# A conditional expert block placed one expert group earlier, in other scratch, and four fewer constant products

## The chip, the cores and the metric

The kernel runs on one core of a Trainium2 chip. The metric is the device time of one execution in microseconds (us). The engines of a core are named as in the profile: PE is the matrix engine (PEld its weight loads), DVE the vector engine, ACT the scalar engine, POOL the general engine and SP the engine that issues nearly all transfers (DMAs). A "q" behind a name is that engine's instruction sequencer.

## The reference, cut to what matters

One decoder layer: a layer norm, a mixer (two branches, gated and summed), a second norm, and a mixture of experts over 256 tokens. The experts stand in 4 groups of 8, and each token goes to two of them. The end of the layer is what this case is about:

```python
for gi in range(N_GROUPS):
    hid = (jax.nn.silu(jnp.einsum("td,edf->tef", t, expert_w_gate[gi]))
           * jnp.einsum("td,edf->tef", t, expert_w_up[gi]))
    hid = hid * combine[:, gi, :, None].astype(hid.dtype)
    y = y + jnp.einsum("tef,efd->td", hid, expert_w_down[gi])
...
h = layer_norm(DEEPNORM_ALPHA * h + ffn, ln2_g[i], ln2_b[i])
```

D_MODEL is 1024 and the inner width of an expert 256, in float32. So each of the 32 experts has 3 MB of weights: gate and up (1 MB each) and down (1 MB).

## The kernel before, in words

The first part of the program (to about 330 us) is the mixer and the router. The second part handles the experts. Each expert gets a row of slots for the tokens that were sent to it, and the experts are worked on four at a time: `units` has eight groups of four, and `four(u)` is called for u = 0 to 7 (the sixth group is u = 5, the seventh u = 6, the last u = 7).

In `four(u)`, `gate_up` (L1273) multiplies the first 32 slots of four experts at once by their gate and up weights (tile `gu`). The four experts alternate matrix by matrix, so the fourth matmul already needs the last of the four experts. `activate` (L1304, L1305), `turn` (L1312, L1313) and `down` (L1322, tile `dn`) follow, and `scatter` (L1334) adds the result to the four output tiles `y`.

Three kinds of work are conditional. If an expert of a group has more than 32 tokens, a second pass is made over its slots 33 to 64 (`tc.If(most > QC)`, L1394 and L1440). If any expert has more than 64 tokens (`CAP`), `overflow_all()` computes the rest in a loop over all experts, with weights loaded once more into a tile `ow` and normed tokens in a tile `hT` (L1450). A branch is decided at run time by each engine for itself. The program has a path for each outcome: where a block is skipped, the engine runs a short path that adds to the semaphores what the block would have added.

Weights come in on one queue, issued by SP in the order in which the program's builder placed them; PE, ACT, DVE and POOL have their order written by hand. Every transfer counts on one of eight semaphores in turn (DMAHW0 to DMAHW7). `load_gu` and `load_dn` take their buffers in rotation through `unit`: seven buffers for `gu`, seven for tag `rd`, which is shared by the `dn` tiles, by `ow`, by `gb` (the broadcast rows of the last norm) and by the result `o`. A tile that is taken earlier moves every later tile to the next buffer. `lt` holds three scratch buffers `wr0` to `wr2`; the gathered slots `xs` of even groups lie in `wr0`, those of odd groups in `wr1`.

Behind u = 6 follow `second_rows()` (four products of L783 and four copies of L1465, which spread the norm's gain and offset over the partitions) and `warm_up(ident, NW3, "pwm3")` (L1082): NW3 products of the identity with itself, whose result nobody reads. Each is two matmuls in the trace.

Of the kernel before, what the change touches and what calls it, by code (L numbers as in the profile page):

```python
# [8 lines left out]
F32R = mybir.dt.float32r  # L9
# [8 lines left out]
P = 128  # L18
D = 1024
KT = 8  # L20
# [21 lines left out]
RT_AT = 2  # L42
XR_AT = (0, 6)
NW2 = 13
NW3 = 18
LN_EPS = 1e-5
RMS_EPS = 1e-6
ALPHA = 2.0 ** 0.25
# [3 lines left out]
def f32(ap):  # L52
    return ap.bitcast(F32)
# [24 lines left out]
def block_kernel(ctx: ExitStack, tc: tile.TileContext, io, out, dbg=None):  # L78
# [17 lines left out]
    lt = ctx.enter_context(late_cm)  # L96
# [713 lines left out]
    def unit(tag, name):  # L810
        order = gu_order if tag == "gu" else dn_order
        k = order[taken[tag] % len(order)]
        taken[tag] += 1
        return pools[k].tile([P, 4096 if tag == "gu" else 2048], F32, name=name, tag=tag, bufs=order.count(k))

    def load_gu(*es):

        for e in es:
            if e < NE:
                raw[e] = [unit("gu", f"gu{e}").rearrange("p (a k f) -> p a k f", a=2, k=KT), None]  # L820
                for a_, nm in enumerate(("expert_w_gate", "expert_w_up")):
                    S.dma_start(raw[e][0][:, a_], io[nm][e].rearrange("(p k) f -> p k f", k=KT))

    def load_dn(*es):

        for e in es:
            if e < NE:
                raw[e][1] = unit("rd", f"dn{e}").rearrange("p (r d) -> p r d", r=2)
                S.dma_start(raw[e][1], io["expert_w_down"][e].rearrange("(p r) d -> p r d", r=2))
# [301 lines left out]
    def gather(c, k, tag):  # L1131

        pt = pm(tag, f"px{c}{k}").rearrange("p (k s) -> p k s", k=2)
        for i in range(2):
            px[c, k + i] = pt[:, i, :]
            for n in "hl":
                for t in range(2):
                    one_part(c, k + i, n, t)
# [7 lines left out]
    def gathered(c, k, eng):  # L1146
        affine(XS[:, k, c * NT:(c + 1) * NT], px[c, k], k, eng)
# [3 lines left out]
    NQ = len(units)  # L1151
# [10 lines left out]
    def slots(u, i, eng, part=0):  # L1162

        e, w = units[u][i], QC
        if i == 0:
            xsd[u, part] = f32(lt.tile([P, 1024], F32R, name=f"xs{u}{part}", tag=f"wr{(u + part) % 2 if u + part else 2}").rearrange("p (k s) -> p k s", k=KT))
        off_ = slot_at(e, eng) if e else 0
        win = XS[:, :, bass.ds(off_ + part * w, w)] if e else XS[:, :, part * w:part * w + w]
        (A.copy if eng is A else V.tensor_copy)(xsd[u, part][:, :, w * i:w * i + w], win)
# [37 lines left out]
    def rest():  # L1207

        for i in range(2):
            pt = pm("ty"[i], f"pg1s{i}")  # L1210
            row(pt, 0, i, True, True)
            for t in range(2):
                x_ = h1[t][:, i * 512:(i + 1) * 512]
                V.tensor_tensor(x_, x_, pt, op=ALU.mult)
        gap(1)

        t0 = rt("mrk0", 2, NE, at=at_pos)
        V.scalar_tensor_tensor(t0, rk, 1.0, asb, op0=ALU.add, op1=ALU.mult)
        V.tensor_scalar_add(mrk, t0, -1.0)


        ge, gp = r2("ge", NG), r2("gp")
        V.tensor_sub(ge, gl, bc(gm, [P, 2, NG]))
        A.activation(ge, ge, AF.Sigmoid, scale=-1.0)
        ws_ = []
        for i in range(2):
            w_ = r2(f"w{i}")
            A.activation(w_, dm, AF.Sigmoid, scale=(1.0, -1.0)[i])
            ws_.append(w_)
        A.activation(r2("warmed"), dm, AF.Silu)  # L1230

        for i in range(2):
            q, a = rt(f"qr{i}", 2, NE, at=at_q2 + 2 * NE * i), r2(f"rs{i}")
            V.scalar_tensor_tensor(q, rk, 1.0, AA[:, i], op0=ALU.add, op1=ALU.mult)
            V.tensor_reduce(a, q, axis=AX.X, op=ALU.add)
            for t in range(2):
                V.tensor_scalar(rhs[:, 2 * i + t, :], iot[:, :CAP], a[:, t, :], None, op0=ALU.is_equal)
        V.reciprocal(ge, ge)
        V.tensor_scalar_add(ge, ge, -1.0)
        V.tensor_reduce(gp, ge, axis=AX.X, op=ALU.add)  # L1240
        V.reciprocal(gp, gp)
        for i, w_ in enumerate(ws_):
            V.tensor_mul(w_, w_, gp)
            V.tensor_mul(CW[i], AA[:, i], bc(w_, [P, 2, NE]))

        V.tensor_add(cov, CW[0], CW[1])
        V.scalar_tensor_tensor(cov, rk, float(CAP), cov, op0=ALU.is_ge, op1=ALU.mult)
# [20 lines left out]
    def gate_up(u, part=0):  # L1268

        pgd[u, part] = pm("g", f"pg{u}{part}")  # L1270
        for k in range(KT):
            for e, c in cols_of(u):
                T.matmul(pgd[u, part][c, :], xsd[u, part][:, k, c], raw[e][0][:, :, k, :], start=k == 0, stop=k == KT - 1)  # L1273

    def weigh():

        pt = pm("y", "pcs")
        for o, c0 in ((0, 0), (NQ, QC)):
            for i in range(2):
                for t in range(2):  # L1280
                    for c in range(4):
                        T.matmul(pt[QC * c:QC * c + QC, o:o + NQ], rhs[:, 2 * i + t, c0:c0 + QC], CW[i][:, t, c::4], start=t + i == 0, stop=t + i == 2)
        V.tensor_copy(cs, pt[:, :2 * NQ])
        both = glp.tile([P, 512], F32, name="hd", tag="gl", bufs=1).rearrange("p (i r s) -> p i r s", i=2, r=2)
        hd.extend(both[:, i] for i in range(2))

    def ranks():
        prk = pm("t", "prk")
        for t in range(2):
            T.matmul(prk[:NE, t * P:(t + 1) * P], mrk[:, t, :], idb, start=True, stop=True)  # L1290
        A.copy(rkT, prk[:NE, :NT])

    def scatter_map(u, part=0):

        pt = ptd[u, part] = pm("t", f"pt{u}{part}")
        for e, c in cols_of(u):
            T.matmul(pt[c, NT:], bc(idb[:NE, e:e + 1], [NE, QC]), rkT, start=True, stop=True)  # L1297
        V.tensor_scalar(sct[(u + part) % 2], pt[:, NT:], smod[:, part:part + 1], None, op0=ALU.is_equal)  # L1298
# [37 lines left out]
    def residual_add(n, t):  # L1336

        T.matmul(y[t][n], ident, h1[t][:, n * 512:(n + 1) * 512], start=True, stop=False)
        row(y[t][n], 1, n, False, False)
# [40 lines left out]
    def next_slots(u):  # L1380
        for i in range(4):
            slots(u, i, V if i % 2 else A)

    def four(u):

        e0 = units[u][0]
        gate_up(u)
        if u == 0:
            for k, tag in ((0, "t"), (2, "y"), (4, "t"), (6, "y")):
                gather(1, k, tag)  # L1390
                for i in range(2):
                    gathered(1, k + i, A if k % 4 else V)
        most = nc.values_load(cmi[0:1, u:u + 1], engines=three, min_val=0, max_val=NT)
        with tc.If(most > QC):  # L1394
            for i in range(4):
                slots(u, i, V if i % 2 else A, 1)
            gate_up(u, 1)
        if u == 0:
            rest()
        n1 = e0 + 7  # L1400
        load_gu(*((n1, n1 + 1, n1 + 2, n1 + 3) if n1 + 4 < NE - 1 else (n1,)))
        if u == 0:
            for t in range(2):
                for n in range(2):
                    residual_add(n, t)
            load_dn(6)
            weigh()
            ranks()
        if n1 == NE - 1:
            load_dn(NE - 4, NE - 3, NE - 2)  # L1410
        scatter_map(u)
        activate(u)
        turn(u)
        if u + 1 < NQ:
            next_slots(u + 1)
            for n in range(2):
                down(u, n, "yg"[n])
            for n in range(2):
                scatter(u, n)
            second(u, most)  # L1420
        else:
            for n in range(2):
                down(u, n, "yg"[n])
            second(u, most)
            for n in range(2):
                scatter(u, n)
        if n1 + 4 < NE - 1:
            load_dn(n1, n1 + 1, n1 + 2, n1 + 3)
        else:
            load_dn(n1)  # L1430
            if n1 < NE - 1:
                load_gu(NE - 4, NE - 3, NE - 2)
        if u == NQ - 2:
            overflow_all()
            second_rows()
            warm_up(ident, NW3, "pwm3")

# [10 lines left out]
    def overflow_all():  # L1448
        most = nc.values_load(cmi[0:1, 8:9], min_val=0, max_val=NT)
        with tc.If(most > CAP):  # L1450
            ow = unit("rd", "ow")
            hT = f32(lt.tile([P, 1024], F32R, name="hT", tag="wr0").rearrange("p (k s) -> p k s", k=KT))
            for t_ in range(2):
                overflow(t_, hT, ow)

# [80 lines left out]
```

## Time and profile before

| what | us |
|---|---|
| median of 3 runs | 560.68 (558.67 to 561.95) |
| the profiled execution | 558.53 |
| its span, first to last instruction | 556.8 |
| PE busy in the span | 475.9 (85%) |
| DMA from 340 to 520 us, in windows of 10 or 20 us | 394 to 424 GB/s |

The page divides the span into 40 slices, and the views of the trace name each instruction by its line of the kernel, its engine and its tiles. All durations in the text are read from the one profiled execution.

### The profile page before, as it was taken

What the parts mean: (1) busy time and instruction counts of PE and PEld (TensorE: products, weight loads), DVE (VectorE), ACT (ScalarE), POOL (GpSimd) and SP (SyncE); (2) the same over time, 40 slices, a digit from 0 to 9 for tenths busy, and PEclk for the clock granted to TensorE, in tenths of its full rate; (3) what the DMA queues carried; (4) which work ended last, traced back from release to release, by engine and by line L of the source; (5) the groups of instructions that cost most, each with busy time, mean ns of one, the idle gap of its engine ahead of it and who ended that gap; (6) DMA issues with size and microseconds to landing.
All of it is one profiled execution on the core that took longest, in us unless ns stands there. A gap on an engine that the chain in (4) does not pass through costs nothing. (4 is left out here: it accounts for less than half of the span.)

```text
span 556.8 us, 8809 instructions
## 1 busy us (share of the span) xinstructions
PE 475.9 (85%) x3353; PEld 339.4 (61%) x3353; DVE 232.7 (42%) x516; ACT 185.0 (33%) x382; POOL 171.1 (31%) x154
## 2 busy tenths in 40 slices
PE   7898799999998998999799879886879898468681
PEld 4797788899987876789787755441222233222520
DVE  5785825663245433336995756220120101001016
ACT  2554345446545464444353412120210201101100
POOL 7492886745544355445450300000000000000002
PEclk9698999999999999999999899897999788879796
DMA  8553242233432414339879995999999999999922
GB/s 202 122 141 87 64 120 82 78 89 101 126 103 75 112 43 117 111 99 316 285 276 416 406 395 207 419 417 419 419 420 417 422 419 415 421 403 421 414 115 75
DMA packets 74582, 136.35 MB, mean 245 GB/s; under 512 B 9857, under 2 KB 59154, under 8 KB 62242
## 3 DMA queue, kind: packets, MB, share of 16 engines
q1 hardware_dynamic: 72640, 134.26, 65.5%
q10 hardware_dynamic: 1890, 1.39, 0.7%
q8 instruction: 33, 0.54, 0.4%
q14 instruction: 19, 0.16, 0.1%
HBM read 133.54 MB, written 2.10 MB: 244 GB/s over the span
## 5 line engine op out<-in xcount | busy, mean ns | idle before, releaser
L232 POOL TENSOR_TENSOR ws_in<-wr_in,ws_in 128x1024 fp32r<-128x1024 f32 x41 | 99.1, 2421 | 74.4 <-ACT ws_in L231 71.5
L236 PE MATMUL pj<-hTh,ws_in 128*128 128x256 f32 (+1 forms) x352 | 105.9, 302 | 1.7 <-ACT hTh L215 1.0
L238 PE MATMUL pj<-hTh,ws_in 128*128 128x256 f32 (+1 forms) x352 | 102.5, 292 | 0.0
L237 PE MATMUL pj<-hTl,ws_in 128*128 128x256 f32 (+1 forms) x352 | 102.2, 292 | 0.2 <-DVE hTl L216 0.2
L1273 PE MATMUL pg<-gu,xs 128*32 128x512 f32 x640 | 76.0, 604 | 11.1 <-DMA gu<-expert_w_up 7.7
L1493 POOL TENSOR_SCALAR rs<-mv 128x1 f32<-128x1 f32 x2 | 0.4, 221 | 233.4 <-DVE mv L1492 233.4
L236 PEld LDWEIGHTS pj<-hTh,ws_in 128*128 128x128 f32 x352 | 68.1, 194 | 4.0 <-issue 1.4
L237 PEld LDWEIGHTS pj<-hTl,ws_in 128*128 128x128 f32 x352 | 67.8, 193 | 1.5 <-issue 0.9
L238 PEld LDWEIGHTS pj<-hTh,ws_in 128*128 128x128 f32 x352 | 67.6, 192 | 0.8 <-issue 0.7
L1273 PEld LDWEIGHTS pg<-gu,xs 128*32 128x32 f32 x640 | 32.4, 111 | 50.3 <-issue 44.4
L1322 PE MATMUL py<-dn,hd 128*32 128x512 f32 x320 | 46.8, 717 | 12.8 <-DMA dn<-expert_w_down 7.8
L231 ACT CAST ws_in<-wr_in 128x1024 fp32r<-128x1024 f32 x44 | 45.9, 1042 | 3.1 <-DMA wr_in<-w_in 3.1
L1298 DVE TENSOR_SCALAR sc<-pt,smod 128x256 fp32r<-128x256 f32 x10 | 4.8, 484 | 99.0 <-PE pt L1297 99.0
L1326 DVE TENSOR_TENSOR yy<-py,yy 128x512 fp32r<-128x512 f32 x20 | 13.8, 692 | 63.6 <-ACT yy L1325 56.5
L1322 PEld LDWEIGHTS py<-dn,hd 128*32 128x32 f32 x320 | 10.9, 126 | 39.8 <-issue 24.2
L1334 PE MATMUL y<-yy,sc 128*128 128x512 f32 x80 | 25.8, 439 | 4.3 <-ACT yy L1325 3.0
L1304 ACT ACTIVATE gs<-pg 128x256 f32<-128x256 f32 x10 | 3.8, 384 | 76.4 <-PE pg L1273 76.4
L1334 PEld LDWEIGHTS y<-yy,sc 128*128 128x128 f32 x80 | 13.9, 194 | 21.9 <-ACT yy L1325 7.4
L1325 ACT CAST yy<-py 128x512 fp32r<-128x512 f32 x20 | 11.7, 586 | 45.5 <-PE py L1322 44.4
L729 DVE TENSOR_TENSOR_SCAN kp<-kp,one 128x144 f32<-128x144 f32 (+1 forms) x16 | 17.5, 1125 | 14.8 <-ACT kp L724 14.8
L311 DVE SCALAR_TENSOR_TENSOR qkv<-pj,cols,qkv 128x271 f32<-128x271 f32 (+2 forms) x36 | 17.8, 498 | 12.9 <-ACT qkv L309 12.3
L888 POOL TENSOR_TENSOR h<-h,gb 128x512 f32<-128x512 f32 x8 | 12.9, 1645 | 12.9 <-ACT gb L885 12.9
(539 smaller groups left out, 830.1 us busy)
## 6 DMA issues: line engine op xcount, KB each, us to landing
gu<-expert_w_gate SPq DMA_DIRECT2D x32, 1024.0 KB
gu<-expert_w_up SPq DMA_DIRECT2D x32, 1024.0 KB
dn<-expert_w_down SPq DMA_DIRECT2D x32, 1024.0 KB
wr_in<-w_in SPq DMA_DIRECT2D x44, 512.0 KB
wr_o<-w_out SPq DMA_DIRECT2D x8, 512.0 KB
wr_w_branch_dn<-w_branch_dn SPq DMA_DIRECT2D x4, 512.0 KB
wr_w_branch_sb<-w_branch_sb SPq DMA_DIRECT2D x4, 512.0 KB
h<-x SPq DMA_DIRECT2D x2, 512.0 KB
```

Of the source, the lines that this page charges most:

```text
L231: A.copy(wh, raw)
L232: (sub or V).tensor_sub(wl, raw, f32(wh))
L236: T.matmul(pt, lh, rh, start=first, stop=False)
L237: T.matmul(pt, lh, rl, start=False, stop=False)
L238: T.matmul(pt, ll, rh, start=False, stop=last)
L311: V.scalar_tensor_tensor(y[:, s:], pt[:, :L - s], ccol(3 - s, r + j), y[:, s:], op0=ALU.mult, op1=ALU.add)
L729: V.tensor_tensor_scan(k_, k_, bc(one1, [P, n]), 1.0, op0=ALU.mult, op1=ALU.mult)
L888: G.tensor_tensor(x_, x_, gb, op=op)
L1273: T.matmul(pgd[u, part][c, :], xsd[u, part][:, k, c], raw[e][0][:, :, k, :], start=k == 0, stop=k == KT - 1)
L1322: T.matmul(py[c, :], hd[(u + part) % 2][:, r, c], raw[e][1][:, r, n * 512:(n + 1) * 512], start=r == 0, stop=r == 1)
L1326: V.tensor_sub(yy[:, 1, :], py, f32(yy[:, 0, :]))
L1334: T.matmul(y[t][n], sct[(u + part) % 2][:, t * P:(t + 1) * P], yy[:, p_, :], start=False, stop=p_ == 1 and part == 0 and u == NQ - 1)
```

## The change

`overflow_all()` is called at the end of u = NQ - 3 = 5 (behind the sixth group) where it was called at the end of u = 6. Its tile `hT` takes scratch `wr1` where it took `wr0` (behind u = 5, `wr0` already holds the slots of u = 6). NW3 is 14 where it was 18.

```diff
-NW3 = 18
+NW3 = 14
...
             load_dn(n1)
             if n1 < NE - 1:
                 load_gu(NE - 4, NE - 3, NE - 2)
+        if u == NQ - 3:
+            overflow_all()
         if u == NQ - 2:
-            overflow_all()
             second_rows()
             warm_up(ident, NW3, "pwm3")
...
-            hT = f32(lt.tile([P, 1024], F32R, name="hT", tag="wr0").rearrange("p (k s) -> p k s", k=KT))
+            hT = f32(lt.tile([P, 1024], F32R, name="hT", tag="wr1").rearrange("p (k s) -> p k s", k=KT))
```

SP, before: the last loads of weights and the start of the block. The names carry the expert's number (gu31 is gate and up of expert 31), and in brackets stand the semaphores on which a row waits.

```order
L822 DMA gu29_5479<-expert_w_up 128x2048 [waits DMAHW7_49]
L822 DMA gu30_5482<-expert_w_gate 128x2048 [waits DMAHW0_49]
L1440 UNCONDITIONAL_BRANCH
L822 DMA gu30_5482<-expert_w_up 128x2048 [waits DMAHW1_49]
L822 DMA gu31_5609<-expert_w_gate 128x2048 [waits DMAHW2_49,PE_49]
L822 DMA gu31_5609<-expert_w_up 128x2048 [waits DMAHW3_49]
L829 DMA dn28_5612<-expert_w_down 128x2048 [waits DMAHW4_49]
L829 DMA dn29_5614<-expert_w_down 128x2048 [waits DMAHW5_49]
L829 DMA dn30_5616<-expert_w_down 128x2048 [waits DMAHW6_49]
L829 DMA dn31_5750<-expert_w_down 128x2048 [waits DMAHW7_49,PE_49]
L1449 TENSOR_LOAD cmi_3692 [waits DVE_49]
L1450 COMPARE_AND_BRANCH
```

The block stands behind all weights: what SP does there has no load behind it.

SP, changed: first the same place (the last loads ahead of the block), then the end of the skipping path and all that follows it up to the last group.

```order
L822 DMA gu29_5479<-expert_w_up 128x2048 [waits DMAHW7_49]
L822 DMA gu30_5482<-expert_w_gate 128x2048 [waits DMAHW0_49]
L822 DMA gu30_5482<-expert_w_up 128x2048 [waits DMAHW1_49]
L1450 TENSOR_LOAD cmi_3692 [waits DVE_49]
L1451 COMPARE_AND_BRANCH
```

```order
L1451 UNCONDITIONAL_BRANCH [waits DMAHW0_49,DMAHW1_49,DMAHW2_49,DMAHW3_49,DMAHW4_49,DMAHW5_49,DMAHW6_49,DMAHW7_49]
L1450 ISA x2
L829 DMA dn28_5753<-expert_w_down 128x2048 [waits DMAHW2_49,PE_49]
L829 DMA dn29_5755<-expert_w_down 128x2048 [waits DMAHW3_49]
L1394 UNCONDITIONAL_BRANCH
L822 DMA gu31_5750<-expert_w_gate 128x2048 [waits DMAHW4_49,PE_49]
L822 DMA gu31_5750<-expert_w_up 128x2048 [waits DMAHW5_49]
L1441 UNCONDITIONAL_BRANCH
L829 DMA dn30_5757<-expert_w_down 128x2048 [waits DMAHW6_49,PE_49]
L829 DMA dn31_5891<-expert_w_down 128x2048 [waits DMAHW7_49,PE_49]
```

Six transfers of 1 MB (gu31 twice, dn28 to dn31) moved behind the block, and dn28 and dn29 now stand ahead of gu31. With `ow` taken earlier in the rotation, dn30 lies in the buffer of dn24 and so follows the join behind the seventh group (L1441), as dn31 does; before, it lay in that of dn23.

PE, before, from the end of the seventh group's second pass to the block, and changed, from the same place to the last group's first products (`ln` are the products of `second_rows`, `pwm3` the constant ones):

```order
L1334 MATMUL y11_3709<-yy611_5743,sc_3704 128x512 x2
L1440 UNCONDITIONAL_BRANCH
L1440 UNCONDITIONAL_BRANCH [waits PE_49]
L1449 TENSOR_LOAD cmi_3692
L1450 COMPARE_AND_BRANCH
```

```order
L1441 UNCONDITIONAL_BRANCH
L1441 UNCONDITIONAL_BRANCH [waits PE_49]
L783 MATMUL ln220_5894<-RB_96,sel_99 128x256 [waits DVE_49,PE_49,Activation_49]
L783 MATMUL ln220_5894<-RB_96,sel_99 128x256
L1082 MATMUL pwm3_5910<-ident_105 128x128 [waits Activation_49]
L1082 MATMUL pwm3_5910<-ident_105 128x128 x13
L1273 MATMUL pg70_5925<-gu28_5476,xs70_5770 32x512 [waits DMAHW5_49,DMAHW4_49,Activation_49]
L1273 MATMUL pg70_5925<-gu29_5479,xs70_5770 32x512 [waits DMAHW7_49,DMAHW6_49]
L1273 MATMUL pg70_5925<-gu30_5482,xs70_5770 32x512 [waits DMAHW1_49,DMAHW0_49]
L1273 MATMUL pg70_5925<-gu31_5750,xs70_5770 32x512 [waits DMAHW5_49,DMAHW4_49]
```

On PE the branch no longer stands between the seventh group and the norm's rows, and four of the constant products are gone; the last group's fourth matmul waits for gu31 as before.

## Rows read from the trace of the kernel before

**Rows 1.** The page, part 2: GB/s moved in each of 40 slices.

```profile
GB/s 202 122 141 87 64 120 82 78 89 101 126 103 75 112 43 117 111 99 316 285 276 416 406 395 207 419 417 419 419 420 417 422 419 415 421 403 421 414 115 75
```

**Rows 2.** Chain that ended last, 476 us to the end: start, us, what.

```profile
543.15 1.41 PE y L1334 x5
544.56 2.50 DVE st L1490 x4
```

**Rows 3.** PE in order of time, 497 to 545 us: start, us, instruction [idle before <-releaser].

```profile
498.06 1.32 PE L1273 MATMUL pg<-gu,xs 128*32 128x512 f32 x6 [0.40 <-PEq L1440]
502.15 7.03 PE L1273 MATMUL pg<-gu,xs 128*32 128x512 f32 x58 [2.77 <-DMA gu<-expert_w_up]
...
515.18 2.46 PE L1334 MATMUL y<-yy,sc 128*128 128x512 f32 x8
518.79 0.93 PE L783 MATMUL ln<-RB,sel 56*128 56x256 f32 x6 [1.15 <-PEq L1450]
522.98 0.58 PE L783 MATMUL ln<-RB,sel 56*128 56x256 f32 x2 [3.25 <-issue]
523.49 6.38 PE L1082 MATMUL pwm<-ident 128*128 128x128 f32 x36
529.80 7.07 PE L1273 MATMUL pg<-gu,xs 128*32 128x512 f32 x64
...
539.34 3.64 PE L1322 MATMUL py<-dn,hd 128*32 128x512 f32 x32 [0.51 <-ACT hd L1313]
```

**Rows 4.** SP's transfers in order of time, 500 to 552 us.

```profile
501.68 0.48 SPq L822 DMA_DIRECT2D gu<-expert_w_up  x1
509.30 0.33 SPq L822 DMA_DIRECT2D gu<-expert_w_gate  x1
...
510.14 7.95 SPq L829 DMA_DIRECT2D dn<-expert_w_down  x4
550.03 0.35 SPq L1486 DMA_DIRECT2D out<-o  x1
```

**Rows 5.** Line L1450, all engines: count, ns min/median/max, first to last start.

```profile
L1450 SPq EVENT_SEMAPHORE  x8: 17/17/17, 519.2 to 534.4; - x8
...
L1450 DVEq EVENT_SEMAPHORE  x1: 21/21/21, 517.7 to 517.7; - x1
...
L1450 PEldq EVENT_SEMAPHORE  x1: 51/51/51, 518.5 to 518.5; - x1
```

**Rows 6.** SP's own waits, 440 us to the end: total us, times, longest.

```profile
SPq L1450 <- SPq L1450: 15.7, 8, 2.5
```

**Rows 7.** Line L1450 on SP from 519.4 us: the last seven waits.

```profile
L1450 SPq EVENT_SEMAPHORE  x7: 17/17/17, 519.5 to 534.4; - x7
```

**Rows 8.** Line L1449, SP's last instruction behind the skipping path.

```profile
L1449 SPq SEQ_ASSERT  x1: 32/32/32, 534.7 to 534.7; - x1
```

**Rows 9.** Windows: length, busy us of PE, PEld, DVE, ACT, POOL, granted clock, DMA share, GB/s.

```profile
533.90:534.40 0.50, 0.50 (x8) 0.13 (x4) 0.00 (x0) 0.00 (x0) 0.00 (x0) 1.00 0.00 0
...
550.00:550.85 0.85, 0.00 (x0) 0.00 (x0) 0.66 (x3) 0.16 (x1) 0.00 (x0) 0.50 0.00 0
550.85:551.75 0.90, 0.00 (x0) 0.00 (x0) 0.90 (x3) 0.00 (x0) 0.79 (x1) 0.50 0.78 291
```

**Rows 10.** Waits of PE, 470 to 545 us: total us, times, longest.

```profile
PE py L1322 <- DMA dn<-expert_w_down: 7.8, 1, 7.8
```

**Rows 11.** PE in order of time, 375 to 396 us.

```profile
381.10 15.17 PE L1273 MATMUL pg<-gu,xs 128*32 128x512 f32 x121 [4.96 <-DMA gu<-expert_w_up]
```

**Rows 12.** Windows behind three idle stretches of PE, columns as in rows 9.

```profile
381.10:384.50 3.40, 3.40 (x17) 0.90 (x21) 0.00 (x0) 0.00 (x0) 0.00 (x0) 0.50 1.02 424
...
489.60:495.30 5.70, 5.68 (x27) 1.29 (x27) 0.69 (x1) 0.59 (x1) 0.00 (x0) 0.63 1.01 423
...
523.00:527.90 4.90, 4.90 (x22) 4.68 (x22) 0.00 (x0) 0.59 (x1) 0.00 (x0) 0.50 1.02 418
527.90:529.80 1.90, 1.90 (x19) 1.78 (x17) 0.00 (x0) 0.00 (x0) 0.00 (x0) 1.00 1.00 414
```

## The prediction

> **What bounds the kernel now.** I read the page's line of moved bytes first. From about the middle of the span on it stands near 420 GB/s [rows 1]: the eight expert groups run at the pace of their weights. Then the chain that ended last. It starts with the last scatter products on PE at 543.15 and goes through the last norm [rows 2], so what counts is when PE reaches the end of the last group. For that I read PE in order of time [rows 3], backwards: the last down products at 539.34 follow the last gate and up products, which run from 529.80 to 536.87 (7.07 us) without a wait ahead of them. What is ahead of them is PE's own work: 36 constant matmuls for 6.38 us, the norm's rows, 3.25 us of idle time that no semaphore ends ("issue"), and 1.15 us of idle time at the branch of L1450. So at this place PE is the late one.
>
> The transfers were not far off, and SP's view tells how far. SP issued its last weights at 510 to 518 us [rows 4] and then stood in L1450 for 15.7 us, in eight waits [rows 6], the first two ending at 519.2 and 519.5, the last at 534.4 [rows 5, 7]. The front part shows what these waits are: the path that skips the block lets SP wait for all eight transfer semaphores, so each one marks a landing. From 519.5 on there are six steps to 534.4, 2.48 us each, which is 1 MB at 420 GB/s. The wait at 519.5 is on the semaphore of gu30's second half (the last transfer issued ahead of gu31); then land gu31 twice, dn28, dn29, dn30 and dn31. So gu31 was whole at 519.5 + 2 x 2.48 = 524.5, 5.3 us before PE came to it, and dn31 was there at 534.4, 4.9 us before PE needed it. DVE and PE pass the same skipping path on one semaphore each, their own [rows 5]; SP alone pays there, and in the kernel before nothing is queued behind it but the output.
>
> **The change part by part.**
>
> *The branch on PE, moved.* Of PE's path at the end go 1.15 us of branch and, if it goes along with the branch, the idle 3.25 us. They come back behind the sixth group, where PE runs six matmuls at 498.06 and then waits 2.77 us for weights until 502.15 [rows 3]. That wait takes up part of them: at worst the seventh group ends 1.15 + 3.25 - 2.77 = 1.6 us later than 517.64 (515.18 + 2.46), at 519.3.
>
> *Four constant products.* Eight matmuls. At the lower clock 22 of them took 4.90 us (223 ns each), at the full one 17 took 1.90 us (112 ns each) [rows 12]: 0.9 to 1.8 us off PE's path.
>
> *hT in wr1.* No instruction is added. I price it at nothing: the next user of wr1 is the copy of the last group's slots, which is made during the seventh group, and PE comes to them only at 529.80 [rows 3].
>
> *SP's eight waits, moved ahead of six loads.* This is the term that decides. gu30's second half was issued at 501.68 [rows 4]. In the changed kernel SP then enters the skipping path and stays until that transfer lands, at 519.5. The wait costs the transfers ahead of it nothing, since all of them are in the queue. But gu31, dn28 and dn29, which were issued from 509.30 to about 511 and so kept the queue full, can't be issued before 519.5, when the queue is empty. What is queued behind the waiting SP is all the weights that the last group still lacks; the last group's gate and up products wait for gu31, its down products for dn28 to dn31. The steps from 519.5 on:
>
> - From the end of the last wait to the next issue: six more passes through waits already met, and the two instructions of L1449, which ended 0.3 us behind the last wait (534.4 to 534.7) [rows 5, 8]. I take 0.5 us, bounds 0.3 and 1.0.
> - From issue to first packet on an idle queue: the output issued at 550.03 moved nothing up to 550.85, and 291 GB/s from then on [rows 4, 9]. I take 0.9 us, bounds 0.8 and 1.1.
> - Four transfers to the end of gu31, because dn28 and dn29 now go first: 4 x 2.48 = 9.9 us [rows 7].
> - From the last packet to the semaphore: no packet starts from 533.90 on, and the wait ends at 534.4 [rows 5, 9]: 0.5 us.
>
> Together 519.5 + 0.5 + 0.9 + 9.9 + 0.5 = 531.3 for gu31, where it was 524.5. Of these 6.9 us (unrounded), 5.0 are the two transfers put ahead and 1.9 the empty queue. [...]
>
> The seventh group ends at 517.6 to 519.3. The norm's rows (0.93 and 0.58 us [rows 3], with their copies some 2 us), 28 constants (3.1 us at 112 ns, 6.2 at 223) and six matmuls (1.3) follow, so PE is ready at 524 to 529 and waits for gu31. Hence the two savings above are worth nothing: they shorten work ahead of a wait that ends at 531.3 in any case. dn30 and dn31 land 2.5 and 5.0 us behind gu31, at 536.3, still ahead of the down products.
>
> *The last group.* Group seven shows it: six matmuls ahead of the wait, then 58 in 7.03 us [rows 3]. So 531.3 + 7.0 = 538.3 against 536.9: 1.4 us late at the full clock. But PE has then stood idle for 2 to 7 us, 5 to 7 if the constants run at the full clock. Behind idle stretches of 4.96 and 7.8 us [rows 10, 11] and behind the 3.25 us before 522.98 the granted clock was 0.50: for 3.4 us from 381.10, for about 4.2 us from 489.62 (mean 0.63 over 5.7 us), for 4.9 us from 523.00 [rows 12]. Behind 2.77 us at 502.15 the products took their full-clock time. [...] Nothing behind the last group changes.
>
> **The sum**: 1.4 + 2.1 = 3.5 us. The profiled execution took 558.53 us (span 556.8 and 1.7 around it), which gives 562.0. It lies 2.2 us under the median of the runs, 560.68, and the forecast is for the median: 560.7 + 3.5 = 564.2 us.
>
> **The rivals.**
>
> *The idle PE keeps its clock.* For it: 2.77 us did no harm, and how long PE waits depends on how late the seventh group gets. Against it: three longer waits, three drops. Then only 1.4 us are lost: 562.1.
>
> *SP is not held.* The point that decides is whether the eight waits cost SP under 1 us. Then dn28 and dn29 go in behind gu30 and gu31 once its buffer is free, at 509.3, all in a full queue; gu31 lands at 519.5 + 4 x 2.48 = 529.4, its products end 7.0 us later at 536.4, 0.5 us earlier than before: 560.2, not slower (with the clock loss 562.3). Against it: the 15.7 us that the same waits took at the end, with six transfers outstanding; behind the sixth group it would be seven, as seven steps of 2.48 us fit between 502.15, when PE got gu27, and 519.5.
>
> *The gain on PE is paid out.* If gu31 came at 524.5 as before, PE could start there, 5.3 us earlier, and be held only at the down products by dn31, which landed 4.9 us before its use: 560.7 - 4.9 = 555.8. It needs gu31 ahead of dn28 in the queue, and the order on SP is the other way round. [...]
>
> *The clock stays low.* If the last gate and up products run wholly at half the clock, 58 of them take 58 x 0.20 = 11.6 us (17 took 3.40 us [rows 12]) for 7.0: 1.4 + 4.6 = 6.0 us, 566.7.
>
> **How the numbers follow.** The forecast has 0.52 (its own range, from the bounds: 562.9 to 565.3), the kept clock 0.20, SP not held 0.12, the gain 0.05, the low clock 0.11. A measurement of this kernel can tell about 0.5%, 2.8 us, from no change. Slower by more: nearly all of the forecast (0.50) and the low clock, 0.61. Faster by more: the gain, and a little of the third case for a release I have not seen, 0.07. The rest, 0.32, is the same. The range 560.8 to 566.8 leaves out the gain and the lower half of the case in which SP isn't held.
>
> **What would show it.** In the changed profile SP's line of the block has eight waits from about 502 on, the first of some 14 us (gu30's first half, one step of 2.48 ahead of 519.5), the second of 2.5, the others already met; dn28 is issued near 520, and the transfers show an empty stretch of 1.5 to 2.5 us there. PE's constants end before 528, then PE idles for 3 us or more before the bulk of the last L1273 group, "<-DMA gu<-expert_w_up", until about 531.3; the clock is 0.50 in the first 3 to 5 us behind it. I am wrong if SP issues dn28 before 510, if PE goes into the last L1273 group without a wait, or if the seventh group ends so late (behind 524) that it holds up PE itself.

## The result, and the profile after

The changed kernel took 564.90 us (median of 20 runs, 563.38 to 570.08); the kernel before, run beside it, took 559.65 (20 runs). The ratio is 1.0101, with a 95% interval of 1.0082 to 1.0119: slower by 1%, or 5.3 us between the medians. The forecast was 564.2, in a range of 560.8 to 566.8. The profiled executions are 6.7 us apart (spans 563.5 and 556.8), which is more than the medians, since the one of the kernel before (558.53) lies 1.1 us under its median and the one of the changed kernel (565.18) 0.3 over it; what follows takes the 6.7 us of the spans apart.

The line numbers of the changed kernel are one higher behind the edit: the block is L1451, its load of the largest count L1450, the join behind a group L1441. The page's line of moved bytes shows the place at once. Where before the slices near the end stood at 421, 403, 421, 414 [rows 1], two now fall short:

```profile
GB/s 200 120 150 75 76 112 85 104 93 96 129 97 75 85 77 105 113 190 298 297 295 402 427 224 312 416 418 418 421 420 418 419 420 417 420 407 323 379 70 74
```

SP's transfers in order of time, in the changed kernel (against [rows 4]; gu30's second half is the one at 502.04):

```profile
502.04 0.44 SPq L822 DMA_DIRECT2D gu<-expert_w_up  x1
520.93 0.82 SPq L829 DMA_DIRECT2D dn<-expert_w_down  x2
521.84 0.38 SPq L822 DMA_DIRECT2D gu<-expert_w_gate  x1
522.28 0.56 SPq L822 DMA_DIRECT2D gu<-expert_w_up  x1
522.96 1.12 SPq L829 DMA_DIRECT2D dn<-expert_w_down  x2
```

For nearly 19 us SP issues nothing. What it does there is in two views: its waits (total us, times, longest) and the block's line on SP, whole and from the second wait on (count, ns, first to last start):

```profile
SPq L1451 <- SPq L1451: 16.9, 2, 14.5
```

```profile
L1451 SPq EVENT_SEMAPHORE  x8: 17/17/17, 517.6 to 520.5; - x8
```

```profile
L1451 SPq EVENT_SEMAPHORE  x7: 17/17/17, 520.0 to 520.5; - x7
```

The first wait ends at 517.6 after 14.5 us, the second at 520.0 after 2.4 more, and the other six take the half microsecond to 520.5. Before, the same eight waits ran from 519.2 to 534.4 [rows 5 to 7], with nothing behind them but the output. Now six loads of weights stand behind them.

Windows of the changed kernel, columns as in [rows 9]:

```profile
517.00:518.00 1.00, 1.00 (x16) 0.32 (x12) 0.21 (x1) 0.59 (x1) 0.00 (x0) 1.00 0.68 279
518.00:519.00 1.00, 1.00 (x9) 0.25 (x2) 0.49 (x1) 0.11 (x1) 0.00 (x0) 1.00 0.33 139
519.00:519.60 0.60, 0.60 (x4) 0.45 (x4) 0.09 (x1) 0.48 (x1) 0.00 (x0) 1.00 0.14 55
519.60:521.90 2.30, 1.95 (x9) 1.05 (x8) 0.60 (x1) 0.00 (x0) 0.00 (x0) 1.00 0.00 0
521.90:522.00 0.10, 0.10 (x3) 0.10 (x3) 0.00 (x0) 0.00 (x0) 0.00 (x0) 1.00 1.56 164
522.00:523.00 1.00, 1.00 (x9) 0.82 (x8) 0.00 (x0) 0.96 (x3) 0.00 (x0) 1.00 0.56 115
523.00:524.00 1.00, 1.00 (x11) 1.00 (x10) 0.00 (x0) 1.00 (x3) 0.00 (x0) 1.00 1.03 434
...
531.58:538.41 6.83, 3.63 (x20) 1.13 (x24) 0.00 (x0) 0.00 (x0) 0.00 (x0) 0.50 0.89 371
538.41:543.60 5.19, 5.19 (x44) 1.29 (x34) 0.00 (x0) 0.00 (x0) 0.00 (x0) 1.00 0.02 6
```

```profile
517.00:523.00 6.00, 5.65 (x39) 2.99 (x31) 1.38 (x2) 2.14 (x5) 0.00 (x0) 1.00 0.30 97
```

The queue doesn't just stop and start. It fades from 517 on, is empty from 519.6 to 521.9, and is back at its pace only at 523. Over these 6 us it moved 97 GB/s where it moves 418: the hole is worth 6 x (1 - 97/418) = 4.6 us of transfers.

PE in order of time (against [rows 3]):

```profile
503.41 9.34 PE L1273 MATMUL pg<-gu,xs 128*32 128x512 f32 x64 [5.43 <-PEq L1451]
...
518.76 2.48 PE L1334 MATMUL y<-yy,sc 128*128 128x512 f32 x8
521.53 1.17 PE L783 MATMUL ln<-RB,sel 56*128 56x256 f32 x8 [0.30 <-PEq L1441]
522.67 3.39 PE L1082 MATMUL pwm<-ident 128*128 128x128 f32 x28
526.00 1.06 PE L1273 MATMUL pg<-gu,xs 128*32 128x512 f32 x6
534.78 8.82 PE L1273 MATMUL pg<-gu,xs 128*32 128x512 f32 x58 [7.73 <-DMA gu<-expert_w_up]
```

Read backwards: the last gate and up products end at 543.60, 6.7 us later than before (536.87), and that is the whole difference of the spans. They waited 7.73 us for gu31's second half. Their first part then ran at half the clock (granted 0.50 over 531.58 to 538.41, 1.00 behind it): 8.82 us for 58 products, where group seven took 7.03 before. But look at 526.00 too: PE stood ready there 3.8 us earlier than before (529.80). The block on PE now costs 5.43 us behind the sixth group, and between the end of the seventh (521.24) and the last gate and up products there are only 0.30 of idle, the rows and the constants, 4.8 us in all, where it was 12.2. PE did gain; the weights came too late for it.

### The profile page after: what moved, and what is told of

It is laid out like the page before. It is cut to its first block, busy times and chain, and to the rows that moved or that the text cites. A ratio compares the mean times of both kernels' runs of the same rounds, so it can differ in the third digit from the quotient of the medians.

```text
span 563.5 us, 8794 instructions
## 1 busy us (share of the span) xinstructions
PE 476.3 (85%) x3345; PEld 339.8 (60%) x3345; DVE 233.1 (41%) x516; ACT 184.7 (33%) x382; POOL 171.8 (30%) x154
## 5 line engine op out<-in xcount | busy, mean ns | idle before, releaser
L1273 PE MATMUL pg<-gu,xs 128*32 128x512 f32 x640 | 81.0, 641 | 21.2 <-DMA gu<-expert_w_up 12.7
L1273 PEld LDWEIGHTS pg<-gu,xs 128*32 128x32 f32 x640 | 36.3, 117 | 61.5 <-issue 54.3
L1322 PEld LDWEIGHTS py<-dn,hd 128*32 128x32 f32 x320 | 11.3, 126 | 39.6 <-issue 23.8
L1325 ACT CAST yy<-py 128x512 fp32r<-128x512 f32 x20 | 11.7, 587 | 45.4 <-PE py L1322 45.4
```

The lines of the kernel that those rows point to most:

```text
L1322: T.matmul(py[c, :], hd[(u + part) % 2][:, r, c], raw[e][1][:, r, n * 512:(n + 1) * 512], start=r == 0, stop=r == 1)
```

## The experiments

Each was timed against the kernel before on the same chip. The first four share one set of runs of the kernel before (median 560.28), the last four another (560.41), and the result above had a third (559.65), so ratios are the safer comparison from one experiment to another. In microseconds a difference of ratios is given below as its share of 560. The profiled executions also reach the sixth group at times up to 6 us apart; where two of them are compared, it is over stretches that start at the same work.

**gu31 ahead of the three down loads.** The waits stay where the change put them; only the order behind them is turned: the loads of dn28 to dn30 are written further down, and the last two groups are recorded in the written order on all engines, so that SP keeps it.

```diff
-        if n1 == NE - 1:
-            load_dn(NE - 4, NE - 3, NE - 2)
         scatter_map(u)
...
         else:
+            if n1 == NE - 1:
+                load_dn(NE - 4, NE - 3, NE - 2)
             load_dn(n1)
...
-    for u in range(NQ):
+    for u in range(NQ - 2):
+        four(u)
+    sp = tc.manual_schedule(...)
+    sp.__enter__()
+    for u in range(NQ - 2, NQ):
         four(u)
...
+    sp.__exit__(None, None, None)
```

> The changed kernel, with SP's order behind the block set by hand: gu31 (both halves) ahead of dn28 to dn31, as it was before the move; SP is still held by the eight waits. My theory (held queue plus order): gu31 lands two transfers, 5.0 us, earlier (529.7 in place of 534.7 in the trace), the last gate and up products start then, and the time falls by 4 to 5.5 us from the changed kernel's 564.9, to 559.4 to 561. [...] Rival B (the reordering is all of the loss): about 1 us below the kernel before, since four constants are gone, 558.5.

Measured: 559.77 us, ratio 0.9991 (0.9963 to 1.0018). The wait of PE with the last down products, and SP's transfers:

```profile
529.12 7.03 PE L1273 MATMUL pg<-gu,xs 128*32 128x512 f32 x58 [2.43 <-DMA gu<-expert_w_up]
...
538.58 4.20 PE L1322 MATMUL py<-dn,hd 128*32 128x512 f32 x32 [0.51 <-ACT hd L1313]
```

```profile
520.50 0.34 SPq L822 DMA_DIRECT2D gu<-expert_w_gate  x1
520.89 0.42 SPq L822 DMA_DIRECT2D gu<-expert_w_up  x1
521.37 2.12 SPq L829 DMA_DIRECT2D dn<-expert_w_down  x4
```

SP is held as long as in the changed kernel (17.1 us in two waits), but gu31 comes 5.7 us sooner: two transfers of 2.48, and 0.4 by which the hold ends earlier here (520.1 for 520.5). PE waits 2.43 and the products take 7.03: they keep the full clock (granted 1.00 from 526 to 546), though the down products behind them take 4.20 us for 3.64. The order alone is worth 5.1 us by the medians and 6.2 by the ratios (0.0110), and takes the loss away without a gain.

**The block's transfers on GpSimd's queue.** The order stays as the change made it; SP has no transfer in the block and thus nothing to wait for on the skipping path.

```diff
-        S.dma_start(ow[:, :1024], spill[t * P:(t + 1) * P, :])
+        G.dma_start(ow[:, :1024], spill[t * P:(t + 1) * P, :])
...
-                    S.dma_start(ogu[:, i], ...)
+                    G.dma_start(ogu[:, i], ...)
...
-                S.dma_start(odn, ...)
+                G.dma_start(odn, ...)
```

> The changed kernel, with the transfers inside the block issued by POOL in place of SP, so that the path that skips the block holds none of SP's eight waits; SP's order (dn28 and dn29 ahead of gu31) stays. My theory: dn28 is issued near 503 in place of 521, the queue stays full, gu31 lands at 520.0 + 4 x 2.48 = 529.9 in place of 534.7, and the time falls by 4 to 5 us, to 560 to 561. [...]

Measured: 561.75 us, ratio 1.0018 (0.9991 to 1.0044), a little over the 560 to 561 that I expected. SP's transfers (gu30's last half at 503.84), PE's wait, and the window of the same 6 us as above:

```profile
503.84 0.78 SPq L822 DMA_DIRECT2D gu<-expert_w_up  x1
506.09 1.22 SPq L829 DMA_DIRECT2D dn<-expert_w_down  x2
514.90 0.33 SPq L822 DMA_DIRECT2D gu<-expert_w_gate  x1
```

```profile
532.04 7.03 PE L1273 MATMUL pg<-gu,xs 128*32 128x512 f32 x58 [2.94 <-DMA gu<-expert_w_up]
```

```profile
517.00:523.00 6.00, 5.71 (x40) 2.29 (x40) 1.49 (x3) 2.15 (x5) 0.00 (x0) 1.00 1.03 425
```

This execution runs some 2 us late from an earlier wait on (dn27 was issued at 500.19, in the changed kernel at 498.10), so 532.04 is about 530 on the other's scale, 4.8 us sooner. The queue has no hole (425 GB/s for 97), and dn28 and dn29 still go first. GpSimd, which has the block's waits here, reached its branch of the block at 329.1 us in the changed kernel and at 330.3 in the one before, long before these loads were issued. The hold alone is worth 3.2 us by the medians and 4.6 by the ratios (0.0083).

**Both.** The two edits above together.

> Both edits: the block's transfers on POOL, and gu31 ahead of dn28 to dn31. My theory: gu31 lands near 525 as in the kernel before, PE comes to the last gate and up products at about 526 behind rows and constants and finds them there, the down products are then held by dn31 (about 534.9) or start by 536: 3 to 4 us under the kernel before, 555.5 to 556.7. [...] Rival B (order alone): the same as with the order alone, 558.5.

Measured: 556.33 us, ratio 0.9921 (0.9891 to 0.9951), faster than the kernel before, and under the changed one by 8.6 us by the medians and 10.1 by the ratios (0.0180). Taken apart, the two edits sum to 8.3 by the medians and 10.8 by the ratios, so within the intervals they add up, though either one by itself already brings the full clock back behind the wait (granted 1.00 and 7.03 us for the 58 products in both). PE:

```profile
497.43 2.43 PE L1334 MATMUL y<-yy,sc 128*128 128x512 f32 x8
505.19 9.38 PE L1273 MATMUL pg<-gu,xs 128*32 128x512 f32 x64 [5.32 <-PEq L1451]
...
520.57 2.47 PE L1334 MATMUL y<-yy,sc 128*128 128x512 f32 x8
523.33 1.17 PE L783 MATMUL ln<-RB,sel 56*128 56x256 f32 x8 [0.30 <-PEq L1441]
524.47 3.39 PE L1082 MATMUL pwm<-ident 128*128 128x128 f32 x28
527.79 7.07 PE L1273 MATMUL pg<-gu,xs 128*32 128x512 f32 x64
```

PE goes into the last group without a wait. The 5.32 us at the moved block are still there in a kernel that is faster than the one before, so these can't be what made the change slow.

**The change with 18 constants.** Only `NW3 = 14` goes back to 18.

> The changed kernel with 18 constant products as before (one part of the change undone). My theory: PE waits for gu31 in any case, so the constants cost nothing, and the idle stretch gets 0.9 us shorter without saving the clock: 564.9 within 1 us. Rival C (fewer constants let the clock fall, and that is a good part of the loss): 1.8 us or more faster, 563 or less.

Measured: 566.12 us, ratio 1.0117 (1.0074 to 1.0159), not to be told from 564.9. The wait for gu31 is shorter by about what the four products take, and ends when it did, since this execution runs 0.8 us late (dn27 was issued at 498.92, in the changed kernel at 498.10):

```profile
535.60 8.78 PE L1273 MATMUL pg<-gu,xs 128*32 128x512 f32 x58 [6.72 <-DMA gu<-expert_w_up]
```

**The kernel before with 14 constants.**

> The kernel before with 14 constant products for 18; the block stays behind the seventh group. In the trace before, the constants are 36 matmuls of 6.38 us, most of them at half clock, and gu31 is there in time, so TensorE is the bound there: eight matmuls fewer take 0.9 (at the full rate) to 1.8 us (at the half rate) off its way to the last gate/up. My theory: the smaller number is worth a small gain by itself, 0.9 to 1.8 us, so 558 to 559 where the kernel before has 560; the loss of the change is all from the place of the block. Rival: the constants are also what brings the clock back, so that with fewer of them the last gate/up begins at half clock (8 us or more in place of 7.07) and nothing is gained, or something lost.

Measured: 560.51 us, ratio 0.9989 (0.9962 to 1.0016): the 0.9 to 1.8 us that I expected lie inside the interval, and so does nothing at all. In its profile the 28 constants took 5.40 us for the 6.38 of 36 [rows 3], and the products behind them still ran at the full rate (7.07), so the rival has no row for it. The gain stays unproven. The profiled execution is a late one, 564.15 us, and one of its rows bears on the clock: the seventh group's products ran at first at half the clock (granted 0.50) behind a wait of only 2.34 us.

```profile
507.69 8.38 PE L1273 MATMUL pg<-gu,xs 128*32 128x512 f32 x58 [2.34 <-DMA gu<-expert_w_up]
```

**The change with 42 constants.** Only `NW3 = 42`: PE is kept busy through most of its wait.

> The changed kernel with 42 constant products in place of 14: TensorE works through some 6.8 us of the 7.7 us in which it stood idle for gu31. This tests the clock term alone, since gu31 lands when it did. My theory: the clock stays at full, the last 58 gate/up matmuls take 7.0 us as before the change and not 8.8, and the end comes 1.8 us sooner: about 563.1, a ratio of 1.006 to 1.007 to the kernel before. Rival: the half clock there has nothing to do with the idle time (or the products cost as much as they save): 564.9 as the changed kernel, or more.

Measured: 565.12 us, ratio 1.0078 (1.0053 to 1.0103). My theory was half right. PE:

```profile
534.62 7.03 PE L1273 MATMUL pg<-gu,xs 128*32 128x512 f32 x58 [1.82 <-DMA gu<-expert_w_up]
...
544.08 5.34 PE L1322 MATMUL py<-dn,hd 128*32 128x512 f32 x32 [0.51 <-ACT hd L1313]
```

```profile
544.60:549.50 4.90, 4.81 (x32) 1.06 (x24) 0.69 (x1) 0.61 (x2) 0.00 (x0) 0.65 0.01 3
```

The 58 products are back at 7.03 us, 1.8 less, as expected. But the granted clock now falls behind them (mean 0.65 over 544.60 to 549.50), and the last down products take 5.34 us for 3.64 [rows 3]: 1.7 of the 1.8 is paid a few microseconds later. The medians agree (565.12 and 564.90), and the ratios (1.0078 and 1.0101) don't rule it out.

**Both edits, with 4 constants.**

> The kernel of the third run (the block's transfers on GpSimd's queue and gu31 ahead of dn28 to dn30), with 4 constant products in place of 14. There the last gate/up began at 527.79, right behind the constants, with no wait for gu31, so these now lie on the way: 20 matmuls of 0.121 us fewer are 2.4 us. My theory: the last gate/up begins at 525.4 to 526 (gu31 is about due then), and the end comes 1.8 to 2.4 us sooner: 554 to 554.5 where the third run had 556.3. Rival: gu31 lands later than that, or without constants the clock falls, and the gain is under 1 us.

Measured: 556.87 us, ratio 0.9919 (0.9890 to 0.9949): no gain over 14 constants, where I expected 554 to 554.5. PE:

```profile
518.65 2.46 PE L1334 MATMUL y<-yy,sc 128*128 128x512 f32 x8
...
525.18 7.03 PE L1273 MATMUL pg<-gu,xs 128*32 128x512 f32 x58 [0.39 <-DMA gu<-expert_w_up]
...
534.64 5.52 PE L1322 MATMUL py<-dn,hd 128*32 128x512 f32 x32 [0.51 <-ACT hd L1313]
```

The gate and up products end at 532.21, with 14 constants at 534.86. But this execution is 1.9 us ahead before the constants begin (the seventh group's last scatter starts at 518.65, there at 520.57), so the ten fewer constants brought 0.7 us of the 2.2 that they save (1.16 us for 3.39). The rest goes because PE now waits for gu31: the 58 products behind this wait take 7.03 us, as long as all 64 without one (7.07), so the six that were done ahead of it save nothing. Then the clock falls again at the down products (granted 0.51 over 535.2 to 538.2, 5.52 us for 3.64), which costs 1.9. Both halves of the rival hold: put on the third run's times, the 58 products begin at 527.1.

**Both edits, with the block in its old place.** The kernel with both edits, and the call of the block put back; `hT`, which has to follow it, is back in `wr0` too.

```diff
-        if u == NQ - 3:
-            overflow_all()
         if u == NQ - 2:
+            overflow_all()
...
-            hT = f32(lt.tile([P, 1024], F32R, name="hT", tag="wr1").rearrange("p (k s) -> p k s", k=KT))
+            hT = f32(lt.tile([P, 1024], F32R, name="hT", tag="wr0").rearrange("p (k s) -> p k s", k=KT))
```

> The kernel of the third run with the block put back behind the seventh group (14 constants, its transfers on GpSimd's queue, gu31 ahead of dn28 to dn30): what the new place is worth once SyncE no longer waits in it. TensorE stands idle at the skipped block in both places (5.3 us behind the sixth group, 1.15 and 3.25 us behind the seventh). My theory: the place itself is worth little, within 1 us of the third run's 556.3. Rival, by which the move is a gain that the held queue hid: this kernel is 2 us or more slower than the third run, at 558 or above.

Measured: 560.20 us, ratio 0.9983 (0.9957 to 1.0009). My theory, that the place is worth nothing, falls: the same kernel with the block in the new place has 0.9921, and the intervals don't meet. PE with the block in its old place:

```profile
496.22 2.43 PE L1334 MATMUL y<-yy,sc 128*128 128x512 f32 x8
...
503.32 7.03 PE L1273 MATMUL pg<-gu,xs 128*32 128x512 f32 x58 [2.92 <-DMA gu<-expert_w_up]
...
516.35 2.47 PE L1334 MATMUL y<-yy,sc 128*128 128x512 f32 x8
519.95 0.59 PE L783 MATMUL ln<-RB,sel 56*128 56x256 f32 x3 [1.14 <-PEq L1450]
524.07 1.43 PE L783 MATMUL ln<-RB,sel 56*128 56x256 f32 x5 [3.53 <-issue]
525.43 4.95 PE L1082 MATMUL pwm<-ident 128*128 128x128 f32 x28
530.31 7.08 PE L1273 MATMUL pg<-gu,xs 128*32 128x512 f32 x64
```

Against the same rows with the new place: from the sixth group's last scatter (498.65) to the end of the seventh's gate and up products (510.35) it takes 11.7 us here, and 14.7 there (499.86 to 514.57). From the seventh's last scatter (518.82) to the last gate and up products (530.31) it is 11.5 here, and 4.75 there (523.04 to 527.79). The new place costs 3.0 us and gives 6.7: 3.7 us, and the ratios differ by 0.0062, 3.5 us. The stall of some 5 us is nearly the same in both places. In the new one it covers a wait for weights that is there anyway (2.92), and its half clock (granted 0.50 there from 504 to 508) falls on one group's products (64 in 9.38 us for 7.07) in place of rows and constants that nothing covers (granted 0.50 here from 522 to 528). This kernel also tells what the two edits, the written order and the 14 constants are worth without the move: nothing clear of noise against the kernel before (0.9983).

## Why the prediction was right

**SP's hold** was the deciding step, and it stood: eight waits, the first of 14.5 us, the second of 2.4, six met at once; dn28 issued at 520.93. Undoing it by the other queue, with everything else left, gave 3.2 to 4.6 us back (medians and ratios).

**The order in the queue** stood too: dn28 and dn29 ahead of gu31 were put at 5.0 us, and turning the order moved gu31 by 5.7 and the time by 5.1 to 6.2.

**gu31's landing** was mis-sized: 531.3 forecast, 534.7 read. The second wait ended at 520.0 and not at 519.5 (0.5; dn27 had gone out 0.3 later as well). From there to the next issue it took 0.9 and not 0.5. The largest part, 2.4, lies between this issue and gu31's landing: 13.7 us where I had 0.9 + 9.9 + 0.5 = 11.3. I had let the empty queue cost only the time with no packets, and brought it back at full pace with the first one; the rows show a queue that fades for 2.6 us and takes another microsecond to come back, a hole of 4.6 us for my 1.9. The first packet itself came about where I had put it: nothing moved from the start of the issue at 520.93 until 521.9, 1.0 us for my 0.9. From the end of that issue, 0.34 us later, it is about 0.6 us.

**The seventh group** ended at 521.24, outside my 519.3 at worst. The stall at the moved block is 5.43 us and not 4.4, and it brought the half clock with it (granted 0.52 over 503.41 to 507.90; 64 products in 9.34 us, for 7.07 in the last group before), which I had left out. It cost nothing, since the wait for gu31 was still 7.7 us long.

**The clock** stands in the sum with 2.1 us, for a wait of 5 to 7. No run shows that figure; in its place the products behind the wait of 7.73 us took 8.82 - 7.03 = 1.8 longer. So the term was near for the products, but filling the wait (42 constants) only moved it to the down products. So it is no price that belongs to this wait alone. Nor does the length of the wait decide: behind 2.43 and 2.94 us the gate and up products kept the full clock, and behind 2.34 us in the run of the kernel before with 14 constants they didn't (8.38 us).

**The sum** was 3.5 us; the medians show 5.3 and the profiles 6.7. That the predicted time came out only 0.7 us off is in part luck: the kernel before ran 1.0 us faster in these runs than in the three that I started from. The direction and the mechanism hold; the size was too small by about a third against the medians, and by half against the profiles.

**The rivals.** The kept clock: no, not at 7.7 us. SP not held: no. The clock staying low: no, it came back to 1.00 at 538.41. *The gain on PE* was no rival but the other half of the change: its condition, gu31 in time, was not met, and with both edits that meet it the time is 556.33. That is close to the 555.8 that I had worked out, but not by that way: PE came to the last products at 527.79, behind its constants, and the down products weren't held by dn31. The old place shows what the gain consists of: 6.7 us given at the end, 3.0 taken behind the sixth group.

The prediction only supposed that the idle 3.25 us at the end go along with the branch. They did, and a stall stood again behind the sixth group, longer: 5.43 us for 1.15 and 3.25. Of the 5.43, 4.40 lie in PE's branch itself, and while it lasts (498.6 to 503.05) the two queues that the page lists as "instruction" move one packet and two (packets, MB, share):

```profile
L1451 PEldq COMPARE_BRANCH  x1: 4403/4403/4403, 498.6 to 498.6; - x1
```

```profile
q8 instruction: 1, 0.02, 1.6%
q14 instruction: 2, 0.02, 0.9%
```

In the kernel before, the same branch took 0.23 us, and one packet and two again were moved in the idle time at the norm's rows (519.7 to 523). What holds PE in the branch is not shown: the profile doesn't say for which engine a packet was, and no run changed only where the code lies.

What stays open is when the clock falls. The short works between the last gate and up and the last down products look alike in all these kernels; behind them the granted clock stayed at 1.00 in the changed kernel and with both edits (3.64 us for the down products), and fell with 42 constants (mean 0.65, 5.34 us) and with 4 (0.51, 5.52 us). With gu31 first it reads 1.00 from 538 to 544, and the down products took 4.20 us all the same. Not tested by itself is `hT` in `wr1`; it moves with the block in every run.

## What to carry to other kernels

A conditional block that is never entered can still cost its engines' queues (here SP stood in it for 16.9 us): look at what the skipping path waits for on the engine that issues the transfers, and at what is queued behind it. A block with transfers belongs on a queue on which nothing urgent follows, and then its place can be chosen for the engine that stalls there, best on top of a wait that exists anyway (3.7 us between the two places here). When a queue is let run dry, price the hole by the bytes that don't move from the first fading to the full pace (4.6 us here, where 2.3 had no packet), and look which load goes first behind it.

## What the runs showed of the hardware

- The queue that ran dry lost 4.6 us of transfers though no packet ran for some 2.3 us only (519.6 to about 521.9): it moved 279, 139 and 55 GB/s in the windows before, and 115 in the one from 522 on, against 418. With gu31 first, the same 6 us moved 119 GB/s on average, a hole of 4.3 us.
- PE's idle time at the skipped block was 4.99 to 5.71 us behind the sixth group, in one piece at the branch (seven kernels), and behind the seventh 1.14 or 1.15 at the branch and 2.95 to 3.53 a few products later (three kernels).
- In the last two groups the 58 products behind a wait for the fourth expert's weights took 7.03 us at the full clock, and all 64 without a wait 7.07: the six done ahead saved nothing.
- With 42 constants, which kept PE busy through most of its wait (1.82 us of it left for 7.73), the 58 products behind it took 7.03 us at a granted 1.00, and the clock then fell for the down products instead (mean 0.65 over 544.60 to 549.50): 1.7 of the 1.8 us were lost there (one profiled execution).
